# Normalised rows stored early, their gain and bias applied later in DRAM's copy, and 28 products of a constant ahead of everything

## The chip, the cores and the metric

The kernel runs on one core of a Trainium2 chip. A core has TensorE (PE: matrix products and transposes; PEld is its weight load), VectorE (DVE), ScalarE (ACT) and GpSimd (POOL), and DMA queues issued by SyncE (SP) and ScalarE. The metric is device time in microseconds, the median of several runs. One execution was also taken by the hardware profiler.

## The reference

One layer of a hybrid decoder trunk in fp32, for 1024 tokens of width 1024 and 16 meta tokens ahead of them:

```
h = layer_norm(concat(meta, x), in_ln_g, in_ln_b)
z = h @ w_in + b_in            # q | k | v | conv value and gate | merge gates
A = attention(q, k, v) @ w_attn_proj          # window 128, 16 meta keys, sinks
C = silu(LN(dwconv31(c_val * sigmoid(c_gate)))) @ w_conv_proj
mixed = sigmoid(g_A) * A + sigmoid(g_C) * C
h = LN(alpha * h + mixed @ w_out)             # alpha = 2 ** 0.25
f = (gelu(g) * u) @ w_down,  u | g = dwconv3(h @ w_up)
out = LN(alpha * h + f)
```

`alpha * h` in the second layer norm is the residual this case is about: the normalised input times gain, plus bias, all times alpha.

## The kernel before

All products are made from split operands: a number is written as hi + lo in a reduced format (fp32r), and hi·hi + hi·lo + lo·hi are three passes of TensorE. `product` (L309, L312, L313) records most of them; `z_first` (L515) the first ones, with `raw=True` (L512) as one fp32 product of unsplit operands.

**Input stage.** The tokens are taken in groups: `tokens` for statistics (meta; x tiles 0, 1; tiles 2 to 4; tiles 5 to 7) and `GT` for columns (0: meta, x0, x1; 1: x2 to x4; 2: x5 to x7). For each group: `stat` (bn_stats, L405, or `half_stat`, L417) on DVE; `table` (L424) on ACT; `newton` (L430 to L433) on DVE; `norm` writes xn (DVE L443 or ACT L445); `turns` transposes 128 x 128 pieces on PE (L463); `scaled` applies gain and bias from PSUM into `tm` on ACT (L469); `parts` splits `tm` into hi (cast, L479) and lo (subtraction, L484 on DVE or L482 on POOL). The split halves live in RHO and RHC. `z_first` then forms three column tiles of z: index 0 is k, 1 is v, 2 is q's first; `evac` takes them out of PSUM. `wsplit0` splits their weights (L491, L493). Three helpers, `dv`, `ac`, `pe`, chain the instructions in the order in which they are written, so the text of this stage is the order of each of these engines. Everything else is put in order by a planner that simulates the program and takes, of what is ready, the instruction of lowest rank (`rank`, `tc.cur_priority`). Loads and stores by `load` go to SP's queue, `store` to ACT's.

**Residual.** `norm` notes its tile in `later`. `residual` (L271, L272) later does two instructions for each x tile, still in SBUF, with the rows' mean and reciprocal deviation and with gb (gain and bias spread over all partitions, scaled by alpha, L269), and stores it to `h0d` in DRAM. The x tiles belong to the pool `start`. When it closes, the pools of convolution and attention take the same space; `cin` (written at L668, the input of the convolution) is the first of them.

**Convolution, attention, gates** fill 65 to 430 us, with `z_tile` on PE.

**Merge stage** (L1084 to L1094), from 431 to 523 us: for each of 8 values of m and 4 groups of columns g, PE makes two products of 12 passes, branch 0 (PSUM tag mm, three banks) and branch 1 (tag t, two banks). `merge` multiplies each by its loaded gate (L1084, L1085), adds (L1086) and splits the sum (ACT L1093, DVE L1094). POOL splits the next weights (L285) once in each m and a second time at two of them. **Output projection:** `out_rows` loads rows of `h0d` and adds them to the product with w_out, in the order of tiles 3, meta, 7, 2, 6, 0, 4, 1, 5.

Of the kernel before, what the change touches and what calls it, by code (L numbers as in the profile page):

```python
# [29 lines left out]
P = 128  # L30
D = 1024
# [32 lines left out]

RK_TURN, RK_SPLIT, RK_EVAC, RK_START, RK_QKV, RK_RESID, RK_ATT = 450, 500, 600, 1000, 10000, 20000, 30000
RK_CLN, RK_OSPLIT, RK_Z, RK_CONV, RK_PROJ = 38000, 39000, 40000, 60000, 70000

# [34 lines left out]
def tile_hybrid_layer(  # L102
# [89 lines left out]
    for j in range(NB):  # L192
        with rank((10, 11, 15, 17, 18, 20, 21, 22)[j]):
            load_x(j)
# [27 lines left out]
    qb = const.tile([P, 4], F, name="qb")  # L222
    nc.vector.tensor_scalar(qb, colA[:, 0:4], HD ** -0.5, None, OP.mult)

    nc.vector.tensor_scalar(colA[:, 10:30], colA[:, 10:30], 0.5, None, OP.mult)
# [3 lines left out]
    nc.vector.tensor_scalar(nsink, sink, -1.0, None, OP.mult)  # L229

# [30 lines left out]

    gb = sp.tile([P, 2, D], F, name="gb")
    load(gb[:, :, :].rearrange("p a b -> p (a b)"), dram(ln0_in, 0, [[0, P], [1, 2 * D]]))
    gb_scaled = []

    def residual(src, mu, rs, n, first, dst):
        if not gb_scaled:
            gb_scaled.append(1)
            after(nc.vector.tensor_scalar(gb, gb, ALPHA, None, OP.mult), last_split[3])  # L269
        src = src[:n]  # L270
        nc.vector.scalar_tensor_tensor(src, src, mu[:n], gb[:n, 0], OP.subtract, OP.mult)  # L271
        nc.vector.scalar_tensor_tensor(src, src, rs[:n], gb[:n, 1], OP.mult, OP.add)  # L272
        load(dst, src[first:n])


# [14 lines left out]
    def weights(shape, fill):  # L290
        fills[0] += 1
        n = fills[0]
        own = n == 3
        raw = sp.tile(shape, F, name="wr3") if own else wraw(shape)
        with rank({1: 14, 2: 13, 3: 16, 4: 23}.get(n, RK_SPLIT)):
            last_fill.append(fill(raw))
        hi, lo = (sp.tile(shape, R, name=t + "3") if own else wsp_p.tile(shape, R, name=t, tag=t)
                  for t in ("whi", "wlo"))
        if n <= 3:
            return hi, lo, raw  # L300
        with rank(RK_SPLIT):
            last_split.append(split(raw, hi, lo, n <= 23))
        return hi, lo
# [86 lines left out]
    tokens = [(-1,), (0, 1), (2, 3, 4), (5, 6, 7)]  # L390
    norms, xns, later = {}, {}, []

# [33 lines left out]
    def newton(t):  # L426
# [6 lines left out]
        dv(stt(m_, mv[:, :, 0], -1.0, r_, OP.mult, OP.mult))  # L433

    def norm(t, j, on_dve):
        x_, n = src_of(j)
        i = tokens[t].index(j)
        mv, t_, r_, m_ = norms[t]
        xns[j] = sp.tile([P, D], F, name="xn", tag="xn", bufs=4) if j >= 0 else xm
        to = xns[j] if j >= 0 else xm[96:]  # L440
        for a in range(0, D, 512):
            if on_dve:
                dv(V.tensor_scalar(to[:, a:a + 512], x_[:, a:a + 512], r_[:n, i:i + 1], m_[:n, i:i + 1], OP.mult, OP.add))  # L443
# [57 lines left out]
    def z_first(g, tiles, *ks, raw=False):  # L501
# [5 lines left out]
        for k in ks:  # L507
            for i in tiles:
# [5 lines left out]
                for j, (w, hl) in enumerate(((hi, 0), (hi, 1), (lo, 0))):  # L514
# [42 lines left out]
    norm(2, 3, False)  # L557
    norm(2, 4, True)
    evac(0, 0)
    parts(0, 5, 6, 7)  # L560
    z_first(0, (1,), 0, 1)
    for k in range(2, 6):
        z_first(0, (1,), k)
        z_first(0, (2,), k - 2)
    turns(1, 0, 1, 2, 3)
    scaled(1, 0, 1, 2, 3)
    wsplit0(0, True)
    z_first(0, (1,), 6)
    z_first(0, (2,), 4)
    z_first(0, (1,), 7)  # L570
    evac(0, 1)
    z_first(0, (2,), 5)
    turns(1, 4, 5, 6, 7)
    z_first(0, (2,), 6, 7)
    evac(0, 2)
    parts(1, 0, 1)
    scaled(1, 4, 5, 6, 7)
    half_stat(3, 5, 0)
    parts(1, 2)
    half_stat(3, 5, 1)  # L580
    parts(1, 3)
    half_stat(3, 6, 0)
    parts(1, 4)
    half_stat(3, 6, 1)
    parts(1, 5)
    half_stat(3, 7, 0)
    parts(1, 6)
    half_stat(3, 7, 1)
    table(3)
    parts(1, 7)  # L590
    newton(3)
    norm(3, 5, True)
    norm(3, 6, False)
    norm(3, 7, True)
    for k in range(8):
        z_first(1, (1, 2), k)
    evac(1, 1, 2)
    z_first(1, (0,), 0, 1)
# [4 lines left out]
    turns(2, 4, 5, 6, 7)  # L603
    scaled(2, 4, 5, 6, 7)
    parts(2, 4, 5, 6, 7, on_pool=(5, 7))
    z_first(1, (0,), 6, 7)
    evac(1, 0)
    for i in range(3):
        z_first(2, (i,), *range(8))
        evac(2, i)  # L610
    first_nm = dv_done[-1]

    tc.cur_priority = RK_RESID + 1000
    vrow = sp.tile([NH, J_LEN], F, name="vrow")
# [7 lines left out]
    wt_c1 = weights([P, KC, P], in_cols(11))  # L622
    tc.cur_priority = RK_RESID
    for src, mu, rs, n, j in later:
        if j >= 0:
            residual(src, mu, rs, n, 0, h0d[2 + j * P:2 + (j + 1) * P, :])
        else:
            residual(src, mu, rs, NMETA, U0, h0d[0:2, :])
    start.close()
# [387 lines left out]


    MX_AT = {2: (RHC, 0), 3: (RHC, 1), 6: (RHC, 2), 7: (RHC, 3), 0: (RHO, 0), 4: (RHO, 1), 1: (RHO, 2), 5: (RHO, 3)}

# [44 lines left out]
    for m in range(KC):  # L1065
# [10 lines left out]
        def merge(g, psa, psb):  # L1076
            a, b = PG[g]
            n = b - a
            with rank(RK_EVAC):
# [13 lines left out]
                last_act = nc.scalar.mul(h, v, 0.5)  # L1093
                nc.vector.scalar_tensor_tensor(mixed2(g, m, 1), v, 0.5, f32(h), OP.mult, OP.subtract)  # L1094
            return ins, last_act
# [12 lines left out]
        if m < 4:  # L1108
            early.append(FA[:, W_AT[m]:W_AT[m] + 1024])
            after(load(early[m], w_out_v[m]), last_gate)  # L1110
    for k in range(4):
        prep_wo(k, early[k])
# [638 lines left out]
```

## Time and profile before

| what | us |
|---|---|
| median of 3 runs (lowest, highest) | 1295.74 (1294.87, 1296.15) |
| the profiled execution, its span | 1294.77, 1293.0 |
| PE, DVE, ACT, POOL busy | 1264.6, 1086.4, 578.5, 66.5 |
| first transpose of an x tile | 11.66 |
| norm of the last group ends (DVE) | 46.50 |
| first product of the convolution's second tile after its wait | 91.23 |

A row of the timeline gives the start, the length, the engine, the line, the operation, what it writes and reads, and in brackets how long the engine was idle before it and what ended that. A row of windows gives, for a stretch, the busy time of PE, PEld, DVE, ACT and POOL, each with its count, then the granted TensorE clock, the share of the DMA engines and GB/s. Matmul records are pipelined: the distance between two starts is the price, not the length.

### The profile page before, as it was taken

Reading aid. Unit: us, or ns where it says so; the run is one execution under the profiler, and the core shown is the slowest. Engines: PE = TensorE matmul, PEld = TensorE weight load, DVE = VectorE, ACT = ScalarE, POOL = GpSimd, SP = SyncE. Lnnn points to the kernel's source line nnn. Section 1 sums busy time; section 2 is a strip of 40 time slices with the busy share of each in tenths; the row PEclk is TensorE's granted clock in tenths of the full one; section 3 lists DMA queues with packets and bytes.
Section 4 is the critical chain, followed back from the end, with each engine's and each line's share of the span. In section 5 each row is a group of like instructions: output and inputs, shape, how many; then the busy total and the mean of one; then the engine's idle time right before and its main releaser. Section 6 shows DMA issues by size and latency. Waiting matters only on the chain.

```text
span 1293.0 us, 21590 instructions
## 1 busy us (share of the span) xinstructions
PE 1264.6 (98%) x8506; PEld 1186.6 (92%) x8506; DVE 1086.4 (84%) x1834; ACT 578.5 (45%) x1049; POOL 66.5 (5%) x35
## 2 busy tenths in 40 slices
PE   5999999999999999999999999999999999999997
PEld 5889999999999999788899999999999997788886
DVE  7888999999979676637899989988889876987697
ACT  4422244545554222345565554554455543535330
POOL 2200000001112232000000000000000000000000
PEclk9999999999999999999999999999999999999999
DMA  6265743433255565222135555453454566989712
GB/s 247 82 237 139 184 119 88 109 88 99 68 135 162 157 168 134 75 79 98 66 131 181 198 192 191 176 205 121 158 209 158 192 228 243 392 288 359 259 67 81
DMA packets 96008, 212.10 MB, mean 164 GB/s; under 512 B 10771, under 2 KB 35923, under 8 KB 95650
## 3 DMA queue, kind: packets, MB, share of 16 engines
q1 hardware_dynamic: 84138, 199.64, 46.3%
q10 hardware_dynamic: 11768, 11.08, 2.6%
q8 instruction: 66, 1.08, 0.4%
q14 instruction: 36, 0.29, 0.1%
HBM read 150.29 MB, written 62.70 MB: 165 GB/s over the span
## 4 chain that ended last, share of the span: by engine, by line
PE 89%; DVE 5%; DMA 4%; ACT 1%; SPq 1%; issue 0%; POOL 0%; DVEq 0%; ACTq 0%
PE px L1472 14%; PE py L1472 9%; PE ps_x L1597 9%; PE ps_z L312 7%; PE ps_z L309 7%; PE ps_z L313 7%; PE ps_z L1597 6%; PE pz L1472 5%; PE pw L1472 5%; PE ps_p L312 2%; PE ps_p L313 2%; PE ps_p L309 2%; PE ps_w L309 2%; PE ps_w L313 2%; PE ps_w L312 2%; PE ps_t L859 1%
## 5 line engine op out<-in xcount | busy, mean ns | idle before, releaser
L677 DVE SCALAR_TENSOR_TENSOR FA<-cin,cols,FA 128x1026 f32<-128x1026 f32 x120 | 154.8, 1300 | 0.2
L309 PE MATMUL ps_z<-RHO,whi 128*128 128x384 f32 (+2 forms) x324 | 104.3, 322 | 2.3 <-DVE cin L668 2.3
L312 PE MATMUL ps_z<-RHO,whi 128*128 128x384 f32 (+2 forms) x324 | 104.9, 324 | 0.0
L312 PE MATMUL ps_z<-RHC,whi 128*128 128x384 f32 (+2 forms) x324 | 104.6, 323 | 0.0
L309 PE MATMUL ps_z<-RHC,whi 128*128 128x384 f32 (+2 forms) x324 | 104.6, 323 | 0.0
L313 PE MATMUL ps_z<-RHO,wlo 128*128 128x384 f32 (+2 forms) x324 | 104.2, 322 | 0.0
L313 PE MATMUL ps_z<-RHC,wlo 128*128 128x384 f32 (+2 forms) x324 | 103.7, 320 | 0.0
L1294 DVE TENSOR_TENSOR RHO<-wr,RHO 128x512 fp32r<-128x512 f32 x94 | 63.5, 684 | 10.9 <-ACT RHO L1293 10.9
L1293 ACT CAST RHO<-wr 128x512 fp32r<-128x512 f32 x94 | 56.6, 619 | 18.6 <-DVE wr L1311 10.1
L282 ACT CAST whi<-wr 128x1024 fp32r<-128x1024 f32 x37 | 38.8, 1050 | 55.9 <-PE ps_z L312 33.5
L309 PEld LDWEIGHTS ps_z<-RHO,whi 128*128 128x128 f32 x324 | 60.9, 188 | 2.9 <-DVE cin L668 2.6
L312 PEld LDWEIGHTS ps_z<-RHC,whi 128*128 128x128 f32 x324 | 60.9, 188 | 0.6
L309 PEld LDWEIGHTS ps_z<-RHC,whi 128*128 128x128 f32 x324 | 60.8, 188 | 0.5
L313 PEld LDWEIGHTS ps_z<-RHO,wlo 128*128 128x128 f32 x324 | 60.9, 188 | 0.3
L313 PEld LDWEIGHTS ps_z<-RHC,wlo 128*128 128x128 f32 x324 | 61.0, 188 | 0.2
L312 PEld LDWEIGHTS ps_z<-RHO,whi 128*128 128x128 f32 x324 | 60.9, 188 | 0.4
L1311 DVE TENSOR_TENSOR wr<-wr 128x512 f32<-128x512 f32 x88 | 60.1, 683 | 0.2
L285 POOL TENSOR_TENSOR wlo<-wr,whi 128x1024 fp32r<-128x1024 f32 x17 | 42.1, 2479 | 186.6 <-ACT whi L282 173.6
L684 ACT ACTIVATE FA<-ps_z,cols 128x386 f32<-128x386 f32 (+2 forms) x48 | 26.1, 544 | 52.7 <-PE ps_z L313 45.0
L1484 ACT COPY FA<-px 128x514 f32<-128x514 f32 (+2 forms) x23 | 13.2, 572 | 81.3 <-PE px L1472 81.3
L1294 DVE TENSOR_TENSOR ws<-wr,ws 128x512 fp32r<-128x512 f32 x60 | 40.6, 684 | 6.1 <-ACT ws L1293 6.0
L1472 PE MATMUL px<-OA,RHO 128*128 128x258 f32 x324 | 43.5, 283 | 0.0
(452 smaller groups left out, 3593.9 us busy)
## 6 DMA issues: line engine op xcount, KB each, us to landing
wr<-in_w_up_dram SPq DMA_DIRECT2D x44, 512.0 KB, 4.1
wr<-in_w_z_dram SPq DMA_DIRECT2D x30, 512.0 KB, 3.3
fd<-FA SPq DMA_DIRECT2D x44, 256.0 KB, 2.4
OB<-in_w_down_dram SPq DMA_DIRECT2D x21, 512.0 KB, 5.0
FA<-sd SPq DMA_DIRECT2D x15, 512.0 KB, 8.8
qt<-qd SPq DMA_DIRECT2D x28, 256.0 KB, 4.1
td<-OB SPq DMA_DIRECT2D x12, 512.0 KB, 3.4
sums<-fd SPq DMA_DIRECT2D x12, 512.0 KB
```

The lines of the kernel that those rows point to most:

```text
L282: ins = nc.scalar.copy(hi, raw)
L285: return (nc.vector if quick else nc.gpsimd).tensor_tensor(lo, raw, f32(hi), OP.subtract)
L309: ins = nc.tensor.matmul(ps, ah, bh, start=i == 0, stop=False)
L312: nc.tensor.matmul(ps, ah, bl, start=False, stop=False)
L313: last = nc.tensor.matmul(ps, al, bh, start=False, stop=i == n - 1)
L677: nc.vector.scalar_tensor_tensor(acc[c], cin[:, j:j + U], wc, acc[c], OP.mult, OP.add)
L684: nc.scalar.activation(t, ps, AF.Tanh, bias=bcol(14 + i), scale=0.5)
L1293: nc.scalar.copy(hi, src)
L1294: ins = nc.vector.tensor_tensor(lo, src, f32(hi), OP.subtract)
L1311: ins = nc.vector.tensor_tensor(*x)
L1472: ins = nc.tensor.matmul(o, x[:, ks], bmat(sub, q, hl, k), start=first and k + j == 0, stop=k == 3 and j == 2, skip_group_check=not first)
L1597: nc.tensor.matmul(banks[i], l[:, ts], r[:, ws], start=first and a and x + k == 0, stop=z and x == len(ops) - 1 and k == 2, skip_group_che ...
```

## The change

- x tiles 2 and 3 are loaded ahead of more weights; the weights come in the order k, q, v (before: v, k, q).
- `norm` stores the normalised tile to `h0d` at once. Tiles 4 to 7 are normalised into the buffer OB instead of a pool of four.
- The three small scalings of the columns (`scalings`) stand behind the second table lookup in DVE's order.
- 28 fp32 products of the 128 x 128 constant `ones` with itself stand first in PE's order.
- q's first group is a raw fp32 product; v's weights are split on ACT and DVE, q's and k's still on ACT and POOL, all later. Groups 1 and 2 of z run in the order of `lagged`: v, and two steps of k behind it q, and two behind that k (for group 2: k, v, q).
- In group 2, casts of four hi parts go from DVE to ACT and four subtractions from POOL to DVE.
- `residual` becomes 16 pieces of 128 x 512 in the merge stage, at the pairs (m, g) of RES_AT: load the rows of `h0d` into one of two buffers, multiply by alpha times gain, add alpha times bias (two DVE instructions), store them back. Pieces 0 and 8 first load and scale half of gb, and also treat the two meta rows. The pool of these buffers, `res`, closes after the merge stage.
- The rank of the bias row's work (`vrow`) goes from 21000 to 20000.

```
-        with rank((10, 11, 15, 17, 18, 20, 21, 22)[j]):
+        with rank((10, 11, 14, 15, 18, 20, 21, 22)[j]):
...
-        with rank({1: 14, 2: 13, 3: 16, 4: 23}.get(n, RK_SPLIT)):
+        with rank({1: 13, 2: 17, 3: 16, 4: 23}.get(n, RK_SPLIT)):
...
-        later.append((x_, mv[:n, i, 0:1], r_[:n, i:i + 1], n, j))
+        load(*((h0d[2 + j * P:2 + (j + 1) * P, :], to) if j >= 0 else (h0d[0:2, :], xm[96 + U0:96 + NMETA])))
...
+    def lagged(g, tiles, steps):
+        for t in steps:
+            for l, i in enumerate(tiles):
+                if 0 <= t - 2 * l < KC:
+                    z_first(g, (i,), t - 2 * l)
+                    if t - 2 * l == KC - 1:
+                        evac(g, i)
...
+    warm = pat.tile([P, 512], F, name="ps_w", tag="o")
+    for i in range(28):
+        pe(nc.tensor.matmul(warm[:, :P], ones, ones, start=True, stop=True))
     stat(0, -1)
...
+    scalings()
     newton(1)
...
-    wsplit0(1, True)
     stat(2, 2, 3)
...
-    parts(0, 0, 1)
+    scaled(0, 5, 6)
+    parts(0, 0)
     stat(2, 4)
-    scaled(0, 5)
-    wsplit0(2, True)
-    scaled(0, 6, 7)
+    table(2)
+    scaled(0, 7)
     z_first(0, (0,), 5, 6, 7, raw=True)
-    table(2)
-    parts(0, 2, 3, 4)
+    parts(0, 1)
     newton(2)
     norm(2, 2, True)
     norm(2, 3, False)
     norm(2, 4, True)
+    z_first(0, (2,), *range(8), raw=True)
     evac(0, 0)
...
+    wsplit0(1)
+    parts(0, 2, 3, 4, 5)
     turns(1, 0, 1, 2, 3)
     scaled(1, 0, 1, 2, 3)
+    z_first(0, (1,), 0, 1, 2, 3)
+    evac(0, 2)
+    parts(0, 6, 7)
+    turns(1, 4, 5, 6, 7)
+    z_first(0, (1,), 4, 5, 6, 7)
+    evac(0, 1)
+    parts(1, 0, 1)
+    wsplit0(2, True)
+    scaled(1, 4, 5, 6, 7)
+    stat(3, 5)
+    parts(1, 2, 3)
     wsplit0(0, True)
...
+    lagged(1, (1, 2, 0), range(9))
     turns(2, 0, 1, 2, 3)
     scaled(2, 0, 1, 2, 3)
-    parts(2, 0, 1, 2, 3, on_pool=(1, 3))
-    z_first(1, (0,), 2, 3, 4, 5)
+    parts(2, 0, 1, 2, 3, hi_act=(1, 3))
+    lagged(1, (1, 2, 0), range(9, 11))
...
+    RES_AT = [(m, g) for m in range(1, 7) for g in ((0, 2) if m < 3 else (0, 1, 2))]
+    def residual(i, behind):
+        h, j = divmod(i, NB)
+        hs = slice(h * 512, (h + 1) * 512)
+        pieces = [((3, 7, 2, 6, 0, 4, 1, 5)[j], P)] + ([(-1, 2)] if j == 0 else [])
+        if j == 0:
+            res_gb[:] = [res_p.tile([P, 2, 512], F, name="gb", tag="gb")]
+            with rank(RK_EVAC):
+                for q in range(2):
+                    load(res_gb[0][:, q], dram(ln0_in, q * D + h * 512, [[0, P], [1, 512]]))
+            behind = nc.vector.tensor_scalar(res_gb[0], res_gb[0], ALPHA, None, OP.mult)
+        gb = res_gb[0]
+        for tile_, n in pieces:
+            rows = h0d[2 + tile_ * P:2 + (tile_ + 1) * P, hs] if tile_ >= 0 else h0d[0:2, hs]
+            t = res_p.tile([P, 512], F, name="res", tag="res", bufs=2)[:n]
+            with rank(RK_EVAC):
+                load(t, rows)
+            for op, q in ((OP.mult, 0), (OP.add, 1)):
+                ins = nc.vector.tensor_tensor(t, t, gb[:n, q], op)
+                after(ins, behind)
+                behind = ins
+            load(rows, t)
...
+            if (m, g) in RES_AT:
+                residual(RES_AT.index((m, g)), last_dve)
```

More of the change, by code (lines that the diff above doesn't have):

```diff
@@ L260, in h0 @@
         return (RHO if k < 4 else RHC)[:, o + a:o + b]
[L262 to L273, printed above, removed]
     tc.cur_priority = RK_QKV
@@ L390, in tile_hybrid_layer @@
     tokens = [(-1,), (0, 1), (2, 3, 4), (5, 6, 7)]
-    norms, xns, later = {}, {}, []
+    norms, xns = {}, {}
     def src_of(j):
@@ L433, in newton, with scalings @@
         dv(stt(m_, mv[:, :, 0], -1.0, r_, OP.mult, OP.mult))
+    def scalings():
+        dv(V.tensor_scalar(qb, colA[:, 0:4], HD ** -0.5, None, OP.mult))
+        dv(V.tensor_scalar(colA[:, 10:30], colA[:, 10:30], 0.5, None, OP.mult))
+        dv(V.tensor_scalar(nsink, sink, -1.0, None, OP.mult))
     def norm(t, j, on_dve):
@@ L558, in tile_hybrid_layer @@
     norm(2, 4, True)
+    z_first(0, (2,), *range(8), raw=True)
     evac(0, 0)
[L560 to L564, printed above, removed]
+    wsplit0(1)
+    parts(0, 2, 3, 4, 5)
     turns(1, 0, 1, 2, 3)
     scaled(1, 0, 1, 2, 3)
-    wsplit0(0, True)
[L568 to L588, printed above, removed]
+    z_first(0, (1,), 0, 1, 2, 3)
[9 more added lines that the diff above has]
+    parts(1, 2, 3)
+    wsplit0(0, True)
+    stat(3, 6)
+    parts(1, 4, 5)
+    stat(3, 7)
+    parts(1, 6, 7)
     table(3)
-    parts(1, 7)
     newton(3)
@@ L594, in tile_hybrid_layer @@
     norm(3, 7, True)
[L595 to L598, printed above, removed]
+    lagged(1, (1, 2, 0), range(9))
     turns(2, 0, 1, 2, 3)
     scaled(2, 0, 1, 2, 3)
-    parts(2, 0, 1, 2, 3, on_pool=(1, 3))
-    z_first(1, (0,), 2, 3, 4, 5)
+    parts(2, 0, 1, 2, 3, hi_act=(1, 3))
+    lagged(1, (1, 2, 0), range(9, 11))
     turns(2, 4, 5, 6, 7)
+    lagged(1, (1, 2, 0), range(11, 12))
     scaled(2, 4, 5, 6, 7)
[L605 to L610, printed above, removed]
+    parts(2, 4, 5, 6, 7, hi_act=(5, 7))
+    lagged(2, (0, 1, 2), range(12))
     first_nm = dv_done[-1]
-    tc.cur_priority = RK_RESID + 1000
+    tc.cur_priority = RK_VROW
     vrow = sp.tile([NH, J_LEN], F, name="vrow")
@@ L622, in tile_hybrid_layer @@
     wt_c1 = weights([P, KC, P], in_cols(11))
[L623 to L628, printed above, removed]
     start.close()
@@ L1015, in tile_hybrid_layer @@
     RT = OB[:, 0:2048]
+    res_stack = ExitStack()
+    res_p = res_stack.enter_context(tc.tile_pool(name="res", bufs=1, side="left", reuse_waits="tile"))
+    RES_AT = [(m, g) for m in range(1, 7) for g in ((0, 2) if m < 3 else (0, 1, 2))]
+    res_gb = []
+    def residual(i, behind):
[19 more added lines that the diff above has]
+            load(rows, t)
     MX_AT = {2: (RHC, 0), 3: (RHC, 1), 6: (RHC, 2), 7: (RHC, 3), 0: (RHO, 0), 4: (RHO, 1), 1: (RHO, 2), 5: (RHO, 3)}
@@ L1110, in tile_hybrid_layer @@
             after(load(early[m], w_out_v[m]), last_gate)
+    res_stack.close()
     for k in range(4):
```

15 lines of the change are left out of this document (7 added, 8 removed).

## The prediction

> **What bounds the kernel now.** I read the page's busy shares first, then TensorE's waits, then the input stage by windows and timeline, then the merge stage.
>
> ```profile
> PE 1264.6 (98%) x8506; PEld 1186.6 (92%) x8506; DVE 1086.4 (84%) x1834; ACT 578.5 (45%) x1049; POOL 66.5 (5%) x35
> ```
>
> TensorE is busy 98% of the span. A change that leaves the products alone can only win where TensorE stands still or runs at a lower clock. All its waits (in total, times, longest) and the clock (the last but two figures of a window):
>
> ```profile
> PE ps_h L463 <- DMA cols<-in_cols_dram: 8.3, 1, 8.3
> PE ps_h L463 <- DVE xn L443: 2.9, 1, 2.9
> PE ps_z L309 <- DVE cin L668: 2.3, 1, 2.3
> PE ps_z L515 <- DVE RHC L479: 1.8, 1, 1.8
> ```
>
> ```profile
> 25.00:26.00 1.00, 0.34 (x1) 0.19 (x1) 0.97 (x3) 0.01 (x1) 0.00 (x0) 0.95 0.00 0
> 26.00:27.00 1.00, 0.93 (x5) 0.86 (x5) 0.95 (x4) 0.00 (x0) 0.00 (x0) 0.50 0.00 0
> ```
>
> Every large wait lies in the first 92 us, which is what the change rewrites. After the 1.8 us pause the clock falls to 0.50. A busy TensorE in this stage is not a full one either: a product held by a semaphore counts as busy. The chain of work shows what holds it (start, length):
>
> ```profile
> 4.96 9.46 DMA x<-in_x_dram
> 83.59 6.48 DMA h0d<-x
> 90.56 0.63 DVE cin L668
> 91.23 0.45 PE ps_z L309
> ```
>
> The first line is the arrival of x; from there the chain is DVE's list. The other three are the second wait: `cin` lies where the x tiles lay, so its first write waits for the last store of the residual, and TensorE waits for a bank.
>
> **The change part by part.**
>
> *28 products of `ones`.* They start when `ones` is there, about 1.1 us, and stand ahead of the first transpose on PE's queue.
>
> ```profile
> 12.14 0.42 PE L463 MATMUL ps_h<-cols,xn 128*128 128x128 f32 x1
> 12.35 0.42 PE L463 MATMUL ps_h<-cols,xm 128*128 128x128 f32 x1
> 18.21 2.00 PE L512 MATMUL ps_z<-FA,wr 128*128 128x272 f32 x8
> 30.04 0.40 PE L515 MATMUL ps_z<-RHC,whi 128*128 128x258 f32 x2
> 30.40 0.41 PE L515 MATMUL ps_z<-RHC,whi 128*128 128x272 f32 x2
> 49.33 1.47 PE L463 MATMUL ps_h<-cols,xn 128*128 128x128 f32 x12
> ```
>
> Transposes come 0.21 us apart early and 1.47/12 = 0.12 later: TensorE starts at half speed, though the windows print 1.00 there. An fp32 product of 272 columns leaves two records, so eight in 2.00 us are 0.50 a product and 128 columns estimate to 0.24 warm, 0.47 cold. 28 end between 1.1 + 6.6 = 7.7 and 1.1 + 13.2 = 14.3 us; with 4 us cold, 8.5 + 19.5 of them, near 9.8. The first transpose will be wanted near 10.6. Cost 0 to 3.7, gain up to the 12 + 12 cold transposes and one product, some 2 to 3 us. Both lie ahead of x tile 4's arrival, which decides (below). I take 0.
>
> *Raw products for q.* Eight products of 0.50 replace eight triples of 0.36 (30.04 to 30.40): +1.1 us of PE, but they need no split, so PE works while DVE forms the parts.
>
> *Order of the input stage.* VectorE, ScalarE, POOL (start, length, what it waited for):
>
> ```profile
> 8.15 0.17 DVE L223 TENSOR_SCALAR qb<-cols 128x4 f32<-128x4 f32 x1 [0.99 <-DMA cols<-in_cols_dram]
> 14.45 1.29 DVE L405 BATCH_NORM_STATS2 st<-x 128x6 f32<-128x512 f32 x2 [0.95 <-DMA x<-in_x_dram]
> 20.97 0.44 DVE L484 TENSOR_TENSOR RHO<-FA,RHO 128x272 fp32r<-128x272 f32 x1
> 21.66 0.44 DVE L484 TENSOR_TENSOR RHO<-FA,RHO 128x272 fp32r<-128x272 f32 x1
> 23.49 1.91 DVE L443 TENSOR_SCALAR xn<-x,r,m 128x512 f32<-128x512 f32 x4
> 30.23 0.36 DVE L479 CAST RHO<-tm 128x384 fp32r<-128x384 f32 x1 [2.77 <-ACT tm L469]
> 31.10 0.35 DVE L479 CAST RHO<-tm 128x384 fp32r<-128x384 f32 x1
> 32.90 2.40 POOL L493 TENSOR_TENSOR wlo<-wr,whi 128x1024 fp32r<-128x1024 f32 x1 [12.12 <-ACT whi L491]
> 32.94 2.77 DVE L484 TENSOR_TENSOR RHO<-tm,RHO 128x384 fp32r<-128x384 f32 x1
> 44.59 1.91 DVE L443 TENSOR_SCALAR xn<-x,r,m 128x512 f32<-128x512 f32 x4
> 12.48 1.03 ACT L491 CAST whi<-wr 128x1024 fp32r<-128x1024 f32 x1
> 57.73 1.23 DVE L285 TENSOR_TENSOR wlo<-wr,whi 128x1024 fp32r<-128x1024 f32 x1 [2.75 <-ACT whi L282]
> ```
>
> ```profile
> 15.00:20.00 5.00, 5.00 (x29) 4.12 (x27) 4.86 (x11) 3.87 (x8) 2.58 (x2) 1.00 1.05 420
> ```
>
> The scalings no longer stand ahead of x tile 1's statistics, where they waited 0.99 for the columns: the first group is 1.2 us early. Then data decides. x tile 3 had landed at 4.96 + 9.46 = 14.42; at 420 GB/s tile 4 (512 KB) follows 1.25 later, 15.7, and as many bytes stand ahead of it after the change. (The removed 1 MB load of gb stood behind all x; the new stores do too.) Statistics 1.5, newton 0.8, one part pair 0.7, norms 1.9: group 1 is normalised at 20.8 instead of 25.40.
>
> From there to group 2's norm DVE has: the wait for ScalarE's cast of the v weights 1.0; their subtraction, moved from POOL, 1.2; six part pairs at 0.69, 4.2; q's low part 0.5; eight pairs at 0.87, 7.0; three statistics 4.5; newton 0.8; norms 1.9. Sum 21.1, end 41.9, against 46.50. To it come POOL's two splits: a DVE subtraction that meets one is held till it ends (2.77 instead of 0.56); statistics were not held. So 0 to 4.8 more, 41.9 to 46.7; before paid such holds too. Behind the norm stands TensorE: its q products come early, its v products wait for parts, and the lagged order leaves many products of group 1 for later, so not all of DVE's lead counts. I take a hold and a half and 1.4 us of gain: between a DVE lead of 4.5, and a loss of 2 where both holds fall full and the clock drops once (half of 3.4 us, as at 25.9).
>
> The Trainium skill (SBUF — State Buffer, section SBUF: two separate sides) has GpSimd and a VectorE instruction with two SBUF inputs exclude each other for a whole instruction. The 2.77 agrees; by it alone both holds are full, and the stage gains nothing.
>
> The part casts on ScalarE instead of POOL's subtractions come last, beside the products of group 2: 0. SP's queue now issues a store of each normalised tile as it appears; behind them stand only weights that are not split before group 2's products run. Cost 0; without that cover, the length of the wait of the store ahead of them.
>
> The skill (TensorE: Matmul & The Clock Gate, section "What's actually happening") wants a whole idle window of about 3.4 us before the clock halves. Here 1.8 us of idleness sufficed, so the trace does not agree, and the starved stretch after 28 us can go cold although no gap is that long.
>
> *Residual leaves the first 90 us.* Nine tiles by two instructions go from DVE, and the store before `cin`:
>
> ```profile
> 87.82 1.12 PE L617 MATMUL ps_v<-tab 128*8 128x400 f32 x4
> ```
>
> ```profile
> L272 DVE SCALAR_TENSOR_TENSOR x<-x,r,gb x8: 1266/1267/1270, 73.2 to 82.1; 128x1024 f32<-128x1024 f32 x8
> ```
>
> 18 x 1.27 = 23 us of DVE hidden beside products, worth nothing itself; the wait is worth 2.3. What could be late next are the bias table's copy and the weights' split; they were ready by 90.6. Gain 2.3, between 0 (another wait in its place) and 3.4 (from 87.8, where the bias row's product comes in between, to 91.23).
>
> *Residual in the merge stage.* Windows of one step of m each (2 and 3), a merge's DVE line, and prices:
>
> ```profile
> 453.91:465.40 11.49, 11.49 (x98) 11.49 (x98) 7.94 (x17) 2.75 (x6) 2.40 (x1) 1.00 0.67 185
> 465.40:476.89 11.49, 11.49 (x98) 11.49 (x98) 9.53 (x17) 3.69 (x7) 4.94 (x2) 1.00 0.66 178
> 454.15 0.42 DVE L1085 SCALAR_TENSOR_TENSOR OB<-OB,ps_p 128x256 f32<-128x256 f32 x1 [0.68 <-PE ps_p L313]
> ```
>
> ```profile
> L1311 DVE TENSOR_TENSOR wr<-wr 128x512 f32<-128x512 f32 x88 | 60.1, 683 | 0.2
> fd<-FA SPq DMA_DIRECT2D x44, 256.0 KB, 2.4
> ```
>
> ```profile
> OB<-sgd SPq DMA_DIRECT2D x21, 256.0 KB, 3.2
> ```
>
> ```profile
> L269 DVE TENSOR_SCALAR gb<-gb x1: 1221/1221/1221, 58.9 to 58.9; 128x2048 f32<-128x2048 f32 x1
> ```
>
> A piece costs DVE 2 x 0.68 = 1.37. DVE is free for 3.5 us of a step, 2.0 in the two steps with a second POOL split. Needed: two pieces in m = 1, 2 (2.7), three later (4.1), and 2.0 more at pieces 0 and 8 (meta rows 1.37, scaling of half of gb 0.6). Short by 1.2, -0.8, 2.1, 4.1, 0.6, 0.6: a backlog up to 7.8 if nothing gives. Banks stand between: branch 1 has two, refilled 4.3 us (three branches of 11.49/8 = 1.44) after a bank is full, and DVE frees it 0.7 after; 3.6 us of backlog cost TensorE nothing. Back to back the instructions overlap by 0.06 (2 us of the backlog), and additions that don't fit can slip behind the merges, as nothing reads the rows till the output projection. So 0 to 4.2 from DVE; I take 0.7. The DMAs (16 loads, 16 stores of 256 KB and the meta rows) add to shares of 0.67: 0.
>
> Sum: 0 - 1.4 - 2.3 + 0.7 = -3.0. The profiled execution took 1294.77 (span 1293.0), 0.97 under the runs' median: 1291.8 for its like, 1292.7 against 1295.74.
>
> **Rivals.** (1) *Same:* group 2's norm comes no earlier, because both of POOL's holds fall full, as the one at 32.94 did, and the merges take 2.1: 0 - 2.3 + 2.1 = -0.2, 1295.5. For it: the chain to 46.5 is DVE's; against: x tile 4 is used 1.5 us earlier. (Full holds are what the rule of the Trainium skill's SBUF page says.) (2) *Slower, by the loop of two buffers:* a piece is loaded (3.2), added to (2.2 with a merge between), stored (2.4), and only then is its buffer loaded again: 7.8 and SP's issues, say 8.5, for two pieces, while m = 3 to 6 ask for two in 11.49 x 2/3 = 7.7. If DVE's fixed order holds a merge behind an addition whose load is late, each of seven loops is late by 0.8 to 1.5; it decides once the sum passes 3.6. With 10 less 3.6, -3.7 + 6.4 = +2.7, and with DVE's own 4.2, +7: 1300, between. For it: DVE is first come in its order; against: the order may place additions late. (3) *Slower at the start:* both holds, a cold window and x tile 4 a microsecond late behind stores: +4 - 2.3 + 1.5 = +3.2, 1298.9.
>
> **How the numbers follow.** A run of this kernel tells 0.2%, 2.6 us, from nothing. Forecast 0.46 (own range 1288.5 to 1293.1), (1) 0.22, (2) 0.20, (3) 0.12. Faster is the first, same the second, slower the last two. Low 1288.5: gains of 4.5 + 2.3; high 1300.5 takes in half of (2).
>
> **What would show it.** Right: no wait for `cin` near 88; transposes 0.12 apart from the first; group 2's norm near 45; TensorE without idleness from 431 to 523. Wrong: ps_p waiting for DVE; adds waiting for `res` loads; cold windows between 28 and 41.

## The result and the profile after

The changed kernel takes 1305.6 us (median of 4 runs, 1304.83 to 1308.69) beside 1295.3 for the kernel before on the same chip: ratio 1.0084, 95% interval 1.0065 to 1.0102. That is 10.3 us slower, above the predicted range. The profiled execution took 1304.83, its span is 1303.0.

Where it went can be read by cutting the span at two products that both kernels have: the first `ps_p` product, which opens the merge stage, and the first `px` product, which opens the up stage. Of the kernel before and of the changed one, the rows of these products (last columns: nanoseconds of one, first and last start):

```profile
L309 PE MATMUL ps_p<-OA,whi x128: 279/281/283, 431.0 to 516.8; 128*128 128x256 f32 x96, 128*128 128x258 f32 x32
L1472 PE MATMUL px<-OC,RHO x324: 276/280/286, 626.7 to 1057.2; 128*128 128x256 f32 x162
```

```profile
L292 PE MATMUL ps_p<-OA,whi x128: 279/281/415, 426.9 to 520.4; 128*128 128x256 f32 x96, 128*128 128x258 f32 x32
L1485 PE MATMUL px<-OC,RHO x324: 276/280/286, 636.6 to 1067.4; 128*128 128x256 f32 x162
```

The merge stage opens 4.1 us earlier, and the up stage 9.9 us later. From the one to the other it was 626.7 - 431.0 = 195.7 us and is 636.6 - 426.9 = 209.7: the stretch with the merges and the output projection lost 14.0 us. Behind it, 1293.0 - 626.7 = 666.3 and 1303.0 - 636.6 = 666.4, nothing changed.

**The input stage after.** Windows (busy times of PE, PEld, DVE, ACT, POOL, then TensorE's granted clock), then rows of PE, DVE and POOL by time (start, length):

```profile
25.00:30.00 5.00, 3.90 (x26) 2.99 (x25) 4.90 (x8) 3.92 (x7) 2.52 (x1) 1.00 0.58 198
30.00:35.00 5.00, 3.49 (x11) 2.67 (x12) 4.86 (x11) 2.27 (x3) 0.27 (x1) 0.83 0.00 0
35.00:40.00 5.00, 4.16 (x19) 3.40 (x18) 4.86 (x9) 0.00 (x0) 2.09 (x1) 0.83 0.35 105
```

```profile
10.52 0.27 PE L454 MATMUL ps_h<-cols,xm 128*128 128x128 f32 x1
10.63 0.27 PE L454 MATMUL ps_h<-cols,xn 128*128 128x128 f32 x1
...
27.56 2.54 DVE L470 CAST RHO<-tm 128x384 fp32r<-128x384 f32 x1
...
32.87 0.35 DVE L470 CAST RHO<-tm 128x384 fp32r<-128x384 f32 x1
...
35.17 2.14 DVE L470 CAST RHC<-tm 128x384 fp32r<-128x384 f32 x1
...
42.58 1.92 DVE L434 TENSOR_SCALAR OB<-x,r,m 128x512 f32<-128x512 f32 x4
...
27.36 2.52 POOL L484 TENSOR_TENSOR wlo<-wr,whi 128x1024 fp32r<-128x1024 f32 x1 [24.05 <-ACT whi L482]
34.73 2.36 POOL L484 TENSOR_TENSOR wlo<-wr,whi 128x1024 fp32r<-128x1024 f32 x1 [4.85 <-ACT whi L482]
```

The transposes stand 0.11 apart from here on (0.21 in the kernel before), so TensorE is warm. Both of POOL's splits hold a DVE cast until about their end (2.54 and 2.14 instead of 0.35), and the clock falls to 0.83 in the starved stretch. Still group 2's norm ends at 42.58 + 1.92 = 44.5 instead of 46.5, and the wait for `cin` is gone from TensorE's waits.

**The merge stage after.** The same columns of windows, then TensorE's waits between 400 and 640 us (in total, times, longest), what the additions waited for, and the chain of work (start, length):

```profile
450.00:475.00 25.00, 25.00 (x212) 25.00 (x211) 22.77 (x43) 7.03 (x14) 7.66 (x3) 1.00 0.85 245
475.00:500.00 25.00, 20.63 (x156) 20.03 (x155) 18.09 (x38) 5.46 (x12) 7.24 (x3) 0.93 0.71 202
500.00:525.00 25.00, 23.84 (x193) 23.11 (x192) 19.18 (x37) 5.46 (x11) 5.27 (x2) 1.00 0.68 186
525.00:550.00 25.00, 21.63 (x99) 14.92 (x98) 16.91 (x28) 7.56 (x12) 2.39 (x1) 0.93 0.42 140
```

```profile
PE ps_p L292 <- DVE OB L1095: 5.1, 4, 2.6
PE ps_w L295 <- DVE OA L268: 3.4, 1, 3.4
```

```profile
L1022 DVE TENSOR_TENSOR res<-res,gb x36: 671/686/2259, 413.6 to 535.7; 128x512 f32<-128x512 f32 x32, 2x512 f32<-2x512 f32 x4
...
its engine sat idle before it (us, times) until:
  DMA res<-h0d: 10.9, 7
```

```profile
485.99 4.96 DMA gb<-in_ln_dram
...
494.25 2.75 DMA h0d<-res
497.02 4.23 DMA res<-h0d
501.34 0.69 DVE res L1022
502.03 0.34 DVE RHC L1104
502.37 0.60 DVE res L1022
503.00 3.60 DMA h0d<-res
506.62 3.45 DMA res<-h0d
510.17 0.69 DVE res L1022
511.11 0.69 DVE res L1022
511.83 3.86 DMA h0d<-res
515.71 3.78 DMA res<-h0d
519.58 2.26 DVE res L1022
```

From 475 us on TensorE stands still for 4.4, 1.2 and 3.4 us of these windows, and two of them run at 0.93. DVE is not short of time there: it works 17 to 19 of 25 us. The chain shows what it stands for: load of a piece, a multiplication and an addition (both called additions here), store, load of the next piece into the same buffer. One round takes 9.6 us (497.02 to 506.62), the next 9.1; with two buffers a round serves two pieces, and the stage asks for two in 11.49 x 2/3 = 7.7. Ahead of that stands the reload of gain and bias at the ninth piece. The split L268 that the output projection needs starts at 529.5, behind an addition (527.5) that waited 2.7 us for its rows; the last additions end at 536, beside the projection.

### The profile page after: what moved, and what is told of

The parts are those of the page before. It is cut to its first block, busy times and chain, and to the rows that moved or that the text cites. A ratio compares the mean times of both kernels' runs of the same rounds, so it can differ in the third digit from the quotient of the medians.

```text
span 1303.0 us, 21780 instructions
## 1 busy us (share of the span) xinstructions
PE 1276.3 (98%) x8554; PEld 1195.9 (92%) x8554; DVE 1085.6 (83%) x1854; ACT 581.9 (45%) x1055; POOL 60.3 (5%) x30
## 4 chain that ended last, share of the span: by engine, by line
PE 87%; DVE 6%; DMA 5%; ACT 1%; issue 1%; SPq 0%; DVEq 0%; ACTq 0%
PE px L1485 14%; PE py L1485 9%; PE ps_x L1610 9%; PE ps_z L295 8%; PE ps_z L292 8%; PE ps_z L296 8%; PE ps_z L1610 5%; PE pz L1485 5%; PE pw L1485 5%; PE ps_w L295 2%; PE ps_w L296 2%; PE ps_w L292 2%; DMA res<-h0d 2%; PE ps_z L506 1%; DMA h0d<-res 1%; PE ps_p L295 1%
## 5 line engine op out<-in xcount | busy, mean ns | idle before, releaser
L268 POOL TENSOR_TENSOR wlo<-wr,whi 128x1024 fp32r<-128x1024 f32 x17 | 43.4, 2550 | 208.6 <-ACT whi L265 199.7
```

The costliest lines, as they stand in the source:

```text
L268: return (nc.vector if quick else nc.gpsimd).tensor_tensor(lo, raw, f32(hi), OP.subtract)
```

## The experiments

First theory (A): the loop of two buffers and the reload make DVE wait, and DVE's fixed order hands the waits to TensorE. Rival (B): the 23 us of additions are too much work for the stage, whatever the loads do. Rival (C): the input stage moved something later on.

The table gives for every run the median and the ratio to the kernel before on the same chip, and from its profile the length from the first `ps_p` to the first `px` product (cut as above, but from the first product's weight load, 0.1 earlier); the merges and the output projection lie in it. A profile is of one run: in lazy and lazy_no_warm of the slowest (1302.6 and 1304.1), in loads_only of the fastest (1289.9).

| kernel | us | ratio [95%] | `ps_p` to `px`, us |
|---|---|---|---|
| before | 1294.3 to 1296.4, by chip | | 195.8 |
| changed | 1305.6 | 1.0084 [1.0065, 1.0102] | 209.8 |
| no_resid | 1291.8 | 0.9975 [0.9965, 0.9985] | 195.8 |
| bufs3_gb_once | 1298.0 | 1.0023 [1.0013, 1.0032] | 199.4 |
| dve_only | 1295.8 | 0.9996 [0.9987, 1.0006] | 198.9 |
| dma_only | 1302.4 | 1.0056 [1.0036, 1.0076] | 206.2 |
| bufs3 | 1300.8 | 1.0059 [1.0041, 1.0076] | 203.4 |
| gb_once | 1308.0 | 1.0110 [1.0094, 1.0126] | 210.8 |
| dma_only_bufs3 | 1297.1 | 1.0022 [1.0009, 1.0036] | 200.1 |
| loads_only | 1292.6 | 0.9974 [0.9964, 0.9984] | 195.9 |
| early | 1299.0 | 1.0039 [1.0026, 1.0052] | 195.8 |
| early2 | 1300.9 | 1.0044 [1.0031, 1.0056] | 195.8 |
| lazy | 1301.0 | 1.0032 [1.0020, 1.0044] | 203.2 |
| lazy_no_warm | 1300.2 | 1.0033 [1.0022, 1.0045] | 205.1 |
| mix_no_warm | 1292.3 | 0.9969 [0.9957, 0.9981] | 196.6 |
| no_resid_no_warm | 1290.8 | 0.9968 [0.9956, 0.9980] | 195.9 |
| before_warm | 1294.9 | 0.9998 [0.9989, 1.0006] | 195.8 |

### What the merge stage loses

**The changed kernel without the merge stage's residual.**

```diff
-            if (m, g) in RES_AT:
-                residual(RES_AT.index((m, g)), last_dve)
```

> Leaves out the residual's gain, bias and alpha: the merge stage has no loads, additions or stores of it, and the rows of h0d stay as the input stage stored them. Theory A (loop of two buffers plus the reloaded constants: waits for DMAs of 10.9 and 3.4 us in DVE's fixed order lose 14 us between the merge stage's start and the up stage) and theory B (some 23 us of added DVE work, lengthened by POOL's holds, are more than the stage has room for, whatever their loads do) both expect about 1305.6 - 14.0 = 1291.5 (1290.5 to 1292.5), with the up stage's first px near 622.6 on the trace and no ps_p wait for OB over 1 us. Theory C (the loss comes from the input stage's new order, which moves something later on as well) expects 1300 or more.

Measured 1291.8, as forecast by (A) and (B), and the stretch is back at 195.8. The residual in the merge stage is the whole loss; theory C falls. What is left, the new input stage, is worth 3.2 us (ratio 0.9975: 1.9 to 4.5).

**Three buffers, and gain and bias loaded once.**

```diff
-            t = res_p.tile([P, 512], F, name="res", tag="res", bufs=2)[:n]
+            t = res_p.tile([P, 512], F, name="res", tag="res", bufs=3)[:n]
-        if j == 0:
+        if i == 0:
             res_gb[:] = [res_p.tile([P, 2, 512], F, name="gb", tag="gb")]
...
-    edge = const.tile([P, 2, KC, 2], F, name="edge")
+    edge = ones[:, 0:32].rearrange("p (a k b) -> p a k b", a=2, k=KC)
```

> Takes away what DVE waits for and keeps its work: three buffers for the residual's rows in place of two (a small tile of another stage is put into one that is done, to make room), and the gain and bias of the first 512 columns loaded and scaled once and used for the second 512 too, so that half of the rows get the wrong gain and bias. Theory A expects the two waits of 10.9 and 3.4 us to go and the time to come near 1291.5 plus at most 2: 1291.5 to 1293.5. Theory B (the added DVE work itself is too much) expects little of it: 1302 to 1305.6, with adds back to back and ps_p still waiting for OB.

Measured 1298.0, between the two: the waits were most of it, but 3.6 us stay in the stretch with the same additions.

**The additions alone, on a tile of zeros.**

```diff
-            t = res_p.tile([P, 512], F, name="res", tag="res", bufs=2)[:n]
-            with rank(RK_EVAC):
-                load(t, rows)
+            t = res_gb[1][:n]
...
-            load(rows, t)
```

> Keeps the 36 multiplications and additions of the merge stage and the two scalings on DVE, but on a tile of zeros that is never loaded: no residual loads, no stores, no loads of gain and bias, so the rows of h0d stay without gain, bias and alpha. Theory A expects the loss gone, as no add can wait for a load: 1291.5 to 1294. Theory B expects the loss to stay: 1302 to 1306.

Measured 1295.8, between the two forecasts, and 3.1 us more in the stretch than without the residual: theory B is not nothing, but it is under a quarter of the 14.0. TensorE's waits and DVE's load there:

```profile
PE ps_p L292 <- DVE OB L1093: 2.0, 2, 1.3
```

```profile
475.00:500.00 25.00, 22.99 (x188) 22.38 (x187) 24.51 (x46) 6.35 (x13) 7.26 (x3) 1.00 0.45 118
```

For 25 us DVE has no room (24.51 busy), and TensorE loses 2.0.

**The loads and stores alone.**

```diff
-            for op, q in ((OP.mult, 0), (OP.add, 1)):
-                ins = nc.vector.tensor_tensor(t, t, gb[:n, q], op)
-                after(ins, behind)
-                behind = ins
-            load(rows, t)
+            after(load(rows, t), behind)
```

> Keeps the loads and stores of the merge stage's 18 pieces and the loads of gain and bias, but leaves out the 36 multiplications and additions, so the rows come back without gain, bias and alpha; DVE waits for no piece. Theories A and B both expect 1291.5 to 1293.5: A because the transfers only cost where DVE stands behind them, B because the work is gone. If the transfers themselves (SP's issues, or the merge's own gate loads queued behind them) are the cause, it stays at 1298 or above.

Measured 1302.4: both theories missed, and the case that neither believed came. With no addition to hold DVE, the transfers cost 10.4 us of the stretch. The waits of DVE for gate loads, of SP for stores and of TensorE, SP's issues by time and the end of the chain of work (start, length):

```profile
DVE OB L1090 <- DMA OB<-sgd: 15.5, 7, 3.4
```

```profile
SPq L113 <- DMA h0d<-res: 37.0, 14, 6.1
```

```profile
PE ps_w L295 <- DVE OA L268: 6.9, 1, 6.9
```

```profile
493.96 0.32 SPq L113 DMA_DIRECT2D h0d<-res  x1
494.32 0.43 SPq L113 DMA_DIRECT2D OB<-sgd  x1
500.85 0.32 SPq L113 DMA_DIRECT2D res<-h0d  x1
501.21 0.43 SPq L113 DMA_DIRECT2D h0d<-res  x1
501.74 0.38 SPq L113 DMA_DIRECT2D OB<-sgd  x1
```

```profile
493.96 6.88 DMA h0d<-res
...
519.40 5.02 DMA OB<-sgd
524.85 1.23 DVE OA L268
526.12 0.79 PE ps_w L295
```

At 494.75 SP has issued a gate load and comes to the load `res<-h0d`, which waits for the store of 493.96; that store lands after 6.88 us, and SP issues nothing until 500.85. The gate load that the next merge needs (`OB<-sgd`) stands behind it and goes out at 501.74. So the loop reaches TensorE by a second way, SP's queue, with no addition on DVE: DVE waits 15.5 us for gate loads, and the split L268 stands behind its late merges. There TensorE waits 6.9 us at once; 0.6 more it waits for a merge, and the window from 525 to 550 us runs at 0.88, an estimate of 3.0 us, together 10.5. Why that store took 6.88 us, where others on this chain took 2.3 to 6.0, was not tested. The Trainium skill (DMA: Bandwidth & Descriptors, section "Anatomy of one DMA — SWDGE (gpsimd) path") says, in a section on transfers that GpSimd issues, that the transfer engines never wait on semaphores; the issuing sequencer does, before it sends. The rows of SP agree.

This made theory D: the loop of store and load through two buffers, in SP's fixed order, is the main loss, by both ways.

**The two parts of the cure one at a time, and the transfers with three buffers.** The edits are those above.

> The whole changed kernel with three buffers for the residual's rows in place of two; gain and bias are still loaded again for the second 512 columns. Three buffers and constants loaded once together came to 1298.0 against 1305.6. Theory D (the loop of store, then load into the same buffer, in SP's fixed order, is the main loss: it makes DVE's additions late and holds the gate loads queued behind it) expects 5.5 to 7.6 of these 7.6 from the buffer alone: 1298 to 1300.5. The rival (the reload of gain and bias stalls DVE once, by 3.4 us, and the rest follows from that) expects 1302 to 1305.5 here.

> The changed kernel with two buffers, but the gain and bias of the first 512 columns loaded and scaled once and used for all (half of the rows so get the wrong gain and bias). Theory D (the two-buffer loop is the main loss) expects 1302 to 1305.6: at most the 3.4 us of the one wait. The rival (the reload is the main loss) expects 1298.5 to 1301.

> The residual's loads and stores alone, without its 36 multiplications and additions on DVE (the rows come back without gain, bias and alpha), now with three buffers. With two it took 1302.4, 10.6 above the kernel without the residual (1291.8), though DVE waited for no piece: it waited 15.5 us for gate loads of the merge. Theory D (a load into a buffer waits at the head of SP's queue for the store out of the same buffer, and the gate loads stand behind it) expects most of it gone: 1292 to 1296. The rival (the transfers themselves are the load, by their issues on SP and their bytes) expects 1299 to 1302.5.

The third buffer alone takes 209.8 to 203.4 in the stretch (6.4 us); its 1300.8 is 0.3 above theory D's range and under the rival's. Loading gain and bias once alone gains nothing (210.8, and 1308.0 is above both ranges): the additions wait 11.9 us for rows, about as before. With the third buffer there, the reload does matter: 203.4 against 199.4. For the transfers alone the third buffer takes 206.2 to 200.1 with the same bytes and issues; 1297.1 lies between the two ranges, less of a cure than D asked for. The 4.3 us left are not the reload's: in dma_only_bufs3 DVE scales gain and bias the second time at 423.5, ahead of the merges. SP still waits 32.7 us for stores there, at the longest 4.9; how much of the 4.3 these waits cost, and how much the bytes, is open.

The whole times understate the third buffer. Behind the stretch, from the first `px` product to the end of the span, the three kernels that have it take 667.9 us, and the same ones with two buffers 666.4 to 666.8. What they share is the small tile `edge`, put into `ones` to make room; whether that is the cause was not tested.

**The loads without the stores.**

```diff
-            after(load(rows, t), behind)
```

> The merge stage's 18 loads of rows and the loads of gain and bias, but no additions and no stores back (the rows stay without gain, bias and alpha). Loads and stores without additions took 1302.4 with two buffers and 1297.1 with three; without any of it 1291.8. If SP's waits for stores are the cost (theory D: a load into a buffer stands at the head of SP's queue until the store out of it has landed, and the gate loads stand behind), nothing is left to wait for: 1291.5 to 1293.5. If the transfers as such are the cost (issues on SP, bytes), half of them cost half: 1296 to 1298.

Measured 1292.6, stretch 195.9: as without the residual, and in theory D's range. But the run shows less than it was built for. Without the stores, all 18 row loads are issued between 405.6 and 441.7 us, ahead of 23 of the merges' gate loads (443.6 to 506.2), while in dma_only they go on until 516.1, between the gate loads. So the same loads cost nothing ahead of the merges; what they would cost beside the gate loads, without stores, isn't shown, and the rival does not fall by this run. What stands against it is the third buffer, which takes 6.1 us off the same transfers.

One of SP's waits here, between 400 and 545 us:

```profile
SPq L113 <- DMA res<-h0d: 22.7, 13, 2.7
```

SP still waits 22.7 us for one row load before the next into the same buffer, and it costs nothing: a queue may wait, as long as what stands behind isn't late. The longest such wait is 2.7 us; for a store in dma_only it was 6.1.

**The sum.** Additions 3.1 (dve_only) and transfers with two buffers 10.4 (dma_only) add to 13.5, of 14.0 measured; with three buffers 3.1 + 4.3 = 7.4, of 7.6 measured. Taken the other way: 6.4 by the third buffer, 4.0 by the reload once that is cured, 3.1 for the additions, 0.5 left. That the sums close is no proof that the parts are the same waits: each kernel gets a new order of DVE and SP from the planner, and dma_only has no reload among its merges (DVE scales gain and bias at 412.8 and 419.2).

### The 28 products

**Added to the kernel before, and removed from the changed kernel without the residual.**

```diff
+    warm = pat.tile([P, 512], F, name="ps_w", tag="o")
+    for i in range(28):
+        pe(nc.tensor.matmul(warm[:, :P], ones, ones, start=True, stop=True))
```

> The kernel before, with the 28 products added in front and nothing else of the change. If they buy nothing: 1294.5 to 1296. If the granted clock at the start is what holds the first stage: 1292 to 1294. Either way it tells how much of the 3.4 us between the kernel before and the kernel without the residual is theirs, and how much the reordered input stage's.

> The kernel without the merge stage's residual (the rows of h0d stay without gain, bias and alpha; it took 1291.8) and now also without the 28 products of the constant tile. If the products buy nothing, as the first stage waits for the tiles of x and for DVE's norms whatever the clock is (the prediction's term of 0), the time stays at 1291 to 1292.5. If the transposes and the first products after them run at half clock without the 28 and the stage ends by them, it is 1293.5 to 1295. If the 28 stand in the way of the first transposes, it is 1288.5 to 1290.5.

Both came out at nothing: 0.9998 of the kernel before with them (0.9989 to 1.0006), and 1291.8 with against 1290.8 without, whose ratios to the kernel before (0.9975 and 0.9968) have overlapping intervals; the 1290.8 is 0.2 under the range for nothing. The window of the kernel before with the products suggests why they don't help there:

```profile
10.00:15.00 5.00, 3.23 (x13) 2.72 (x14) 3.59 (x10) 4.06 (x7) 1.27 (x1) 0.68 1.03 419
```

In the 5 us after the products TensorE stands still a third of the time, for want of normalised tiles (its wait for `xn` is 2.2 us), and the granted clock averages 0.68.

### Where else the residual can go

**In SBUF, right after the first stage** (early): `h0d` isn't stored by `norm` but after a multiplication and an addition on the normalised tiles, ahead of the merge stage by 350 us; gain and bias come in one load. The diff is early's. In early2 DVE's scaling is put behind `last_split[3]` in place of `first_nm`, and the last four tiles come later.

```diff
+    after(nc.vector.tensor_scalar(gb, gb, ALPHA, None, OP.mult), first_nm)
+    for to, j in later:
+        rows = slice(0, P) if j >= 0 else slice(96, 96 + NMETA)
+        t = to[rows] if j >= 0 else xm[rows]
+        for op, q in ((OP.mult, 0), (OP.add, 1)):
+            nc.vector.tensor_tensor(t, t, gb[rows, q], op)
...
```

> The new input stage with its stores, but the residual's gain and bias applied in SBUF to the normalized tiles right after the first stage, before the projection's long run of products ends, and stored once from there: the merge stage carries nothing of it and no row is loaded back. Gain and bias come in one 1 MB load at the start. If the merge stage is the whole loss, the time is that of the kernel without the residual, 1291.8, plus 0 to 1.5 for DVE's 18 additions in the q, k, v stage: 1291.5 to 1293.5, 2 to 4 under the kernel before. If the additions or the 1 MB load cost something in the input stage (the rival: the start's transfers are full, and POOL's holds fall in the same stretch), it is 1294 to 1297.

> Residual applied in SBUF early in the attention's first part, as in the run called early, but DVE's scaling and additions now stand behind the split of the fourth matrix after the start, which they held up there: TensorE stood 5.5 us for that split. The meta rows and the first four tiles come first, the other four, which lie in a tile that is not used again until the merge stage, with lower rank. If that wait was the whole of early's 7.2 over the kernel without the residual, the time is 1292 to 1294. If instead the some 23 us of additions delay the rest as well (the gated inputs of the convolution, due near 83, come near 90 in this order, and TensorE has three banks to wait in), it is 1294 to 1297.

Both missed: 1299.0 and 1300.9. The merge stage is as free as without the residual (195.8 in both), but the stages ahead lose time: the first `ps_p` product comes at 434.2 and 436.8 us, for 429.1 in no_resid. The largest waits of TensorE, of early and then of early2:

```profile
PE ps_z L299 <- DVE wlo L271: 5.5, 1, 5.5
```

```profile
PE ps_z L295 <- DVE cin L667: 4.0, 1, 4.0
```

Ahead of the split, 9 tiles of additions make the split late; behind it, they make the convolution's input late.

**Where the output projection loads the rows anyway** (lazy): two instructions behind a load that is there.

```diff
             load(whole, h0d[u:u + n, :])
+            with rank(RK_TURN):
+                for op, q in ((OP.mult, 0), (OP.add, 1)):
+                    nc.vector.tensor_tensor(whole, whole, gb[:, q], op)
```

> The residual is computed in full, but where the output projection loads each row tile anyway: two operations of DVE on the loaded tile, with gain and bias loaded once in the merge stage. No row is loaded or stored for it. DVE has about 24 of 50 us free between 550 and 600 and 5.6 of 40 between 600 and 640 on the trace without the residual, and each tile costs two times 1.2 us. If the copy through DRAM was the loss, 1292 to 1294, under the kernel before. If the additions themselves are too much where DVE is full (the last four tiles, beside the sums for the up stage): 1294.5 to 1298.

> As lazy, and without the 28 products of the constant tile. These bought nothing in two comparisons (1291.8 with and 1290.8 without them beside the kernel without the residual; 1294.9 with and 1295.1 without beside the kernel before), so the time is lazy's, 0 to 1 less.

lazy missed too: 1301.0, above both ranges. lazy_no_warm came 0.8 under it, 1300.2, as forecast. The merges are free, but the last four row tiles share DVE with the sums for the up stage. A window of lazy and its largest wait of TensorE:

```profile
610.00:630.00 20.00, 16.81 (x69) 13.72 (x70) 17.29 (x29) 6.89 (x17) 0.00 (x0) 0.83 0.21 76
```

```profile
PE ps_h L1254 <- DVE OB L1244: 3.4, 2, 3.1
```

The 5.6 us that DVE has free between 600 and 640 don't take four tiles at 2.4. But a full DVE isn't all of it. Between 540 and 640 us DVE stands 9.9 us, five times, for the row loads (4.4 in mix_no_warm, none in no_resid). On lazy's chain a finished tile's store takes 4.62 us (from 596.75), the row load waiting for it 3.22, and only then come the two instructions (604.74). That is again a loop through two buffers, and the new work stands in its round.

**Half in each place** (mix_no_warm): tiles 0, 1, 4 and 5 as in early behind the fourth split, the other four and the meta rows as in lazy, and no products of `ones`.

```diff
+        if j in (0, 1, 4, 5):
+            later.append((to, j))
+        else:
+            load(*((h0d[2 + j * P:2 + (j + 1) * P, :], to) if j >= 0 else (h0d[0:2, :], xm[96 + U0:96 + NMETA])))
...
             load(whole, h0d[u:u + n, :])
+            if i not in (0, 1, 4, 5):
+                with rank(RK_TURN):
...
```

> Without the 28 products; the residual of the tiles 0, 1, 4 and 5 applied in SBUF in the q, k, v stage behind the fourth split (9.8 us of DVE, in place of 22 in the run called early2), and that of the tiles 3, 7, 2 and 6 and of the meta rows where the output projection loads them. If early2 lost its time to the sheer length of DVE's additions ahead of the convolution's input, half of them fit: 1291 to 1293.5. If any such work there is too much: 1295 or more.

Measured 1292.3 against 1296.4 on that chip: 0.9969 of the kernel before (0.9957 to 0.9981), with the whole residual computed. It beats the kernel before and the changed one. Where lazy stood at 0.83 of the clock, the window now reads

```profile
610.00:630.00 20.00, 20.00 (x113) 16.98 (x112) 16.08 (x31) 8.97 (x22) 0.00 (x0) 1.00 0.10 38
```

and the stretch has 196.6. No row goes through DRAM once more for the residual.

## Why the prediction was wrong

- *28 products: 0.* Right, by both comparisons; the transposes are warm from the first, and the stage ends by the tiles of x and DVE, as it said.
- *Order of the input stage, -1.4, and the wait for `cin`, -2.3.* Together -3.7, measured -3.2 (no_resid). Group 2's norm came at 44.5 for a forecast of near 45. Tiles 2 to 4 were normalised at 20.3 for a forecast of 20.8 (its prices add to 20.6). Both holds fell, 4.0 of the 4.8 us it allowed for, and the clock dipped, the two things it was afraid of, and the gain was there all the same. Of the single terms only the sum was measured. The rule it quoted from the Trainium skill (SBUF — State Buffer, section "SBUF: two separate sides") names, beside instructions with two inputs, those in DVE's fast modes; here two casts with one input were held. The rows fit the rule if these casts run in such a mode, which no row here tells. Rivals (1) and (3) drew slower starts from the holds and did not come.
- *Residual in the merge stage, DVE: 0.7 of 0 to 4.2.* It measured 3.1. The bound was right and the choice too low: it let additions slip behind the merges since nothing reads the rows until the output projection. DVE's order, written ahead, has them between the merges: in the chain above, an addition stands ahead of a merge's L1104.
- *The DMAs: 0.* This is the step that failed. It looked at shares of 0.67 and took the room in them for no cost. What it left out of this term is that a load into a used buffer waits at the head of SP's queue until the store out of it has landed, and that the merges' gate loads stand behind it. The transfers cost 10.4 by themselves, with no addition on DVE, and 4.3 with a third buffer, the bytes and the issues being the same. So 6.1 of the 10.4 are the wait for a buffer; of the 4.3 no run shows the cause.
- *Store on SP: 0.* Right where it was said, in the input stage: no_resid keeps these stores, and the input stage gained. The same thought was not repeated for the stores of the merge stage.
- *Rival (2), the loop of two buffers, +2.7 to +7 at 0.20.* The mechanism was named, its round was put at 8.5 us and is 9.1 to 9.6 in two rounds, and the 10 us of lateness that it worked out at most stand as 10.9 us of waits. Its price was too low: it took 3.6 us off for the banks, while in the rows TensorE waits 5.4 us for merges and then 3.4 for the split L268 behind them, so what the banks bridge seems to be paid at the output projection (not tested apart). And it saw only DVE, not the gate loads behind SP, and not the reload of gain and bias at the ninth piece. With 10.4 in its place and 3.1 for DVE, -3.7 + 13.5 = +9.8, measured +10.3.
- *What would show it.* Of its signs of being right those of the input stage came; all three of being wrong came too.

What stays open: by which of the two ways, late additions on DVE or late gate loads on SP, the 10.4 reach TensorE in the changed kernel itself. There DVE waits for rows and not for gate loads, perhaps since it is late already; dma_only shows that the second way alone is enough, and the first alone was not run. With three buffers both are small: DVE waits 2.1 us for rows and 2.4 for a gate load (bufs3). Whether the same transfers on another engine's queue are harmless wasn't tried.

## What to carry to other kernels

A copy through DRAM in place (load, change, store, load the next into the same buffer) is priced by its round, divided by the buffers, against the pace of the stage, and then by everything that stands behind its loads on the issuing queue. Room in the share of the DMA engines (0.67 before, 0.68 to 0.85 after) doesn't rule it out: look for a wait that can come to the head of an in-order queue, and for the most urgent transfer behind it. And work that was hidden in one stage isn't free in another: the residual's multiplications and additions fitted as a whole in none of the three places tried, but half and half in two of them.

## What was not expected of the hardware

- The instructions of TensorE and DVE ahead of the merges are the same, in the same order, but for up to five of the residual's own at the end of DVE's, in nine of these kernels (the changed one, no_resid, bufs3, gb_once, bufs3_gb_once, dma_only, dma_only_bufs3, loads_only and lazy). Their profiles reach the first `ps_p` product after 426.1 (loads_only) to 431.4 us (lazy), with no_resid at 429.1. In no_resid the clock is 0.80 and 0.85 between 35 and 45 us, in loads_only 0.85 and 0.81 between 30 and 40; what else differs, and whether the place of the cold stretches is the cause, was not tested. So the 4.1 us that the two profiles show for the input stage are one draw, and the 3.2 of the medians is the better figure.
- A store of 256 KB followed by a load into its buffer takes 2.75 + 4.23 to 3.86 + 3.78 us on the chain, about 7 to 7.6, a quarter to somewhat over a third more than the sum of the medians of such transfers in the kernel before (2.4 and 3.2).
- Two buffers and a reload don't add up: loading the constants once gains 4.0 us with three buffers and nothing with two.
